# Column-tiled SSD reads and outputs placed in front of the adaLN units of a hybrid decoder layer

## The chip, the cores and the metric

The kernel runs on one core of one Trainium2 chip, as a single program. The metric is device time in microseconds, the median of the runs made. TensorE (PE in the profile, its weight loads PEld) multiplies, VectorE is DVE, ScalarE is ACT, GpSimd is POOL, and SyncE (SP) issues every transfer. Each engine works through its own queue in order.

## The reference, cut to what matters

One decoder layer is run for 256 prompt tokens and 8 sample sequences of 8 tokens (320 token columns in all). Each layer modulates its input by adaLN: six vectors come from `silu(c) @ w_ada`, with one row of `c` per sequence. The branch that the change touches is the Mamba-2 (SSD) branch:

```
per group g of 8 (8 heads of dim 64, state 128):
  x, B, C = silu(conv4(h @ w_in)) ; dt = softplus(...) ; cs = cumsum(dt * A)
  state read    y_t  = exp(cs_t) * (C_t . state)                      sample sequences: 8 stored states
  in the chunk  y_t += sum_s [ (C_t . B_s) * exp(cs_t - cs_s) * dt_s ] x_s
  state update  state = exp(cs_L) * state + sum_s dL_s x_s B_s^T
  y = (y + d_skip * x) * silu(z) ; rmsnorm per group ; times w_ssd_proj
```

Everything is float32. Large products are made as three single-pass products of a value split into a high and a low part (`fp32r`); small ones, the state reads, the outputs y and the adaLN units among them, are made in plain float32.

## The kernel before, in words

The large products run as a stream of weight halves. A half is a 128x1024 block of one weight array, loaded into a ring of four `raw` tiles (the adaLN weights use the same ring), split by ACT (`whi`, a cast) and DVE (`wlo`, a subtraction), in rings of three each. `quad_mm` takes two halves (a quad) and makes 48 products (`mm`): three matmuls for each of 4 column blocks `mb` and 4 rows `kk`. A stage of 16 quads is `project`, here over `w_sp` (for the first group over `w_gp`); a stage of 4 quads is one block of `w_in`. After each block `mb` of a half, eight times in a quad, `bg.tick()` advances a background generator by one step; a generator that yields n lets n ticks pass. Only TensorE's order is written by hand; the other engines' queues are ordered by a scheduler, and `now(x)` keeps an instruction behind the last TensorE instruction emitted before it.

Every second quad (`ada_every[0] = 2`) one adaLN unit is loaded at the start of the quad and multiplied at its end by `Ada.mm`: 4 matmuls of 128x512 in four column strips of 32 (`tile_position=(0, 32*j)`), after `flush` has transposed (`p`) the results of a finished row.

`ssd_work` is the generator of one group. It starts while the z columns of `w_in` are multiplied (4 quads) and goes on during the following `w_sp` stage of the group before. Its TensorE work stands between ticks: two state reads `inter` (4 strips of 32 each), eight updates `upd`, `cb` (C by B), the transposes `xT` and `bT`, the prompt state `fin` (two matmuls, with `bt`, copied by ACT, and `xL`, made by POOL), and four outputs `y`, one for each pair of heads, in two strips of 64. Before each y, ACT makes the weights of two heads in `weights(h)`: three Relu activations and one Exp, and POOL multiplies by `cb`. In the z stage ACT also evacuates the four products of z as `silu` (`evac_z`); the first products of the following stage need the same four PSUM buffers. Exp and silu stand in different ACT tables, and a change of table is an instruction (`ACT_TABLE_LOAD`).

In the line numbers of the profile: L115 is every matmul, L118 every transpose, L132 the cast `whi`, L106 every two-operand operation of DVE or POOL, L109 every activation, L167 a weight load.

Of the kernel before, what the change touches and what calls it, by code (L numbers as in the profile page):

```python
# [19 lines left out]
NT = 320  # L20
# [40 lines left out]
def hybrid_kernel(tc, ctx, a, o):  # L61
# [71 lines left out]
        return first, tt(eng, lo, src, hi.bitcast(F32), ALU.subtract)  # L133


    class Background:
        def __init__(self):
            self.queue = []
# [2 lines left out]
        def add(self, gen):  # L141
            self.queue.append(gen)

        def tick(self):
            if self.wait > 0:
                self.wait -= 1
                return
            if self.queue:
                try:
                    self.wait = next(self.queue[0]) or 0  # L150
                except StopIteration:
                    self.queue.pop(0)
# [95 lines left out]
    class Ada:  # L248
# [23 lines left out]
                self.loaded.append((c, b0, nb, q, raws))  # L272

        def mm(self):
            self.flush()
            if not self.loaded:
                return
            c, b0, nb, q, raws = self.loaded.pop(0)
            if q == 0:
                t = psum.tile([128, 512], F32, tag="ad", bufs=1, name="ad")  # L280
                self.ps = t
            w = 128 * nb
            m = 2048 // w
            n = m // len(raws)
            for j in range(m):
                T.matmul(self.ps[32 * (j % 4):32 * (j % 4) + 32, :w], c_s[:, m * q + j, :],
                         raws[j // n][:, (j % n) * w:(j % n) * w + w], start=q == 0 and j < 4,
                         stop=q == nb - 1 and j >= m - 4, tile_position=(0, 32 * (j % 4)))
            if q == nb - 1:
                part = stile([128, 512], name="adap")  # L290
                S.copy(part[:, :w], self.ps[:, :w])
                self.parts.append((c, b0, nb, part))
# [31 lines left out]
        T.matmul(ps, wh, xl, start=False, stop=False)  # L324
        T.matmul(ps, wl, xh, start=False, stop=stop)

    def quad_mm(pss, name, xq, first, last, evac, n_ada, apart, later):
        xh, xl = xq
        if n_ada:
            ada.load()  # L330
        for h in range(2):
            wh, wl = stream.take(name + (h,))
            for mb in range(4):
                for k2 in range(2):
                    kk = 2 * h + k2
                    c = k2 * 512 + mb * 128
                    block(pss[mb][:, :NT], wh[:, c:c + 128], wl[:, c:c + 128],
                          xh[:, kk], xl[:, kk], first and kk == 0, last and kk == 3)
                if mb == 0:
                    stream.ahead(1 if apart and last and h == 1 else S_AHEAD)  # L340
                if h == 0 and mb == 1 and later is not None:
                    later()
                if last and h == 1 and evac is not None:
                    evac(mb, pss)
                bg.tick()
        if n_ada:
            ada.mm()

# [3 lines left out]
    def gemm(names, quads, evac, apart=False):  # L352
        pss = [mm_ps() for _ in range(4)]
        n = len(names)
        for q in range(n):
            quad_no[0] += 1
            xq = quads(q) if callable(quads) else quads[q]
            quad_mm(pss, names[q], xq, q == 0, q == n - 1, evac,
                    1 if ada_every[0] and len(ada.units) > 4 and quad_no[0] % ada_every[0] == 0 else 0, apart,
                    (lambda: quads(q + 1)) if callable(quads) and q + 1 < n else None)  # L360


# [601 lines left out]
    def v8(x):  # L964
        return x.rearrange("p (h d) -> p h d", d=64)
# [4 lines left out]
    def ssd_work(W):  # L970
# [19 lines left out]
        xl = stile([64, 512], name="xl")  # L990
        tt(V, v8(xl), v8(ps[0:64]), bc8(dtL_tok[:, hsl]), ALU.mult)
        tt(V, v8(xs_tok[0:64]), v8(ps[0:64]), bc8(dt_tok[0:64, 2, hsl]), ALU.mult)
        yield 4

        psA = ax_ps("inter")
        for hf in range(2):
            mv = stack_v(xl, hf)
            states.read(psA, [cpad[:, 4 * hf + j] for j in range(4)], hf, hf == 0, hf == 1)
            for j in range(4):
                st = states.tiles[4 * hf + j]  # L1000
                tt(G, v8(st), v8(st), bc8(ecs_all[:, hsl, 4 * hf + j]), ALU.mult)
            if hf == 0:
                csb = []
                for i in range(2):
                    t = qtile(name="csb")
                    src = bass.AP(tensor=cs_d.tensor, offset=cs_d.offset + (8 * g + 4 * i) * NT,
                                  ap=[[0, 128], [NT, 4], [1, NT]])
                    now(nc.sync.dma_start(t, src))
                    csb.append(t)
            yield 1  # L1010
            for j in range(4):
                states.update(hf, j, hst[hf][:, j], mv, lambda st, ps: tt(V, st, st, ps, ALU.add))
                yield 1
        inter = stile([128, 512], name="inter")
        tt(V, v8(inter), v8(psA), bc8(ecs_r[:, hsl]), ALU.mult)
        yield 1
        states.store(8)

        ps = ax_ps("cb")
        T.matmul(ps[:, 0:256], Bc[:, 0:128], Cc[:, 0:256], start=True, stop=True)  # L1020
        T.matmul(ps[:, 256:384], Bc[:, 128:256], Cc[:, 128:256], start=True, stop=True)
        wide = W.bcm.rearrange("p a b -> p (a b)")[:, NT * 2 * (g % 2) + NP:NT * 2 * (g % 2) + NP + 128]
        T.matmul(ps[:, 384:448], wide, Cc[:, 256:320], start=True, stop=True)
        cb = stile([128, 448], name="cb")
        tt(V, cb[:, 0:384], ps[:, 0:384], mask[:, 0:384], ALU.mult)
        tt(V, cb[0:64, 384:448], ps[0:64, 384:448], mask[0:64, 384:448], ALU.mult)

        wt = ws[0:64]
        for i in range(2):
            now(tt(V, wt[:, 4 * i:4 * i + 4], csb[i][0:64, :, NP:],  # L1030
                   cs_tok[0:64, 2, 8 * g + 4 * i:8 * g + 4 * i + 4].unsqueeze(2).to_broadcast([64, 4, 64]),
                   ALU.subtract))
        V.tensor_scalar(out=wt, in0=wt, scalar1=0.0, scalar2=None, op0=ALU.min)
        act(wt, wt, AF.Exp)
        tt(V, wt, wt, cb[0:64, 384:448].unsqueeze(1).to_broadcast([64, 8, 64]), ALU.mult)
        yield

        xdt = []
        for tb in range(2):
            ps = ax_ps("xT")  # L1040
            for mb in range(4):
                T.transpose(ps[:, 128 * mb:128 * mb + 128], xs[:, mb, 128 * tb:128 * tb + 128], ident)
            xt = stile([128, 512], name="xdt")
            tt(V, v8(xt), v8(ps), bc8(dt_tok[:, tb, hsl]), ALU.mult)
            xdt.append(xt)
            yield

        ps = ax_ps("bT")
        for tb in range(2):
            T.transpose(ps[:, 128 * tb:128 * tb + 128], Bc[:, 128 * tb:128 * tb + 128], ident)  # L1050
        bt = stile([128, 2, 128], name="bt")
        S.copy(bt, ps[:, 0:256].rearrange("p (a b) -> p a b", a=2))
        xL = []
        for tb in range(2):
            xl = stile([128, 512], name="xL")
            tt(G, v8(xl), v8(xdt[tb]), bc8(dL_tok[:, tb, hsl]), ALU.mult)
            xL.append(xl)
        yield 3
        ps = ax_ps("fin")
        for tb in range(2):  # L1060
            T.matmul(ps, bt[:, tb], xL[tb], start=tb == 0, stop=tb == 1)
            yield
        fs = stile([128, 512], name="fs")
        S.copy(fs, ps)
        nc.sync.dma_start(o["ssm_p"][g], fs)


        def weights(h):
            cbr = csb[h // 4][:, h % 4]
# [6 lines left out]
            tt(G, w, w, cb[:, 0:384], ALU.mult)  # L1076
            return w

        ahead = [weights(0), weights(1)]
        yield 4  # L1080
        for j in range(4):
            if j < 3:
                ahead += [weights(2 * j + 2), weights(2 * j + 3)]

            ps = ax_ps("y")
            w = [ahead.pop(0), ahead.pop(0)]
            for cols, lhs, rhs, first in (
                    (slice(0, 256), xdt[0], lambda e: w[e][:, 0:256], True),
                    (slice(128, 256), xdt[1], lambda e: w[e][:, 256:384], False),
                    (slice(256, 320), xs_tok, lambda e: ws[:, 2 * j + e], True),  # L1090
                    (slice(256, 320), inter, lambda e: sel, False)):
                for e in range(2):
                    h = 2 * j + e
                    T.matmul(ps[64 * e:64 * e + 64, cols], lhs[:, 64 * h:64 * h + 64], rhs(e), start=first,
                             stop=not first, tile_position=(0, 64 * e))
            i = 4 * g + j
            V.scalar_tensor_tensor(out=xs[:, j], in0=xs[:, j], scalar=vec[:, V_DS + i:V_DS + i + 1],
                                   in1=ps[:, :NT], op0=ALU.mult, op1=ALU.add)
            yield 4

    def ssd_finish(W):
        g, xs = W.g, W.xs
# [332 lines left out]
```

## Time and profile before

| | |
|---|---|
| median of 3 runs | 2919.72 us (2915.18 to 2924.14) |
| the profiled execution, its own time | 2921.36 us |
| its span, first to last instruction | 2919.6 us |
| mean granted TensorE clock | 0.995 |
| PE busy | 2867.7 us (98%) |
| DVE, ACT, POOL busy | 1582.2 us (54%), 1237.1 us (42%), 377.5 us (13%) |

TensorE sets the time: whatever lengthens or shortens its queue by a microsecond, or lets it wait, shows in the total. The other engines have spare time on average, but their queues are in order, so that one late instruction holds back what stands behind it.

### The profile page before, as it was taken

What the parts mean: (1) busy time and instruction counts of PE and PEld (TensorE: products, weight loads), DVE (VectorE), ACT (ScalarE), POOL (GpSimd) and SP (SyncE); (2) the same over time, 40 slices, a digit from 0 to 9 for tenths busy, and PEclk for the clock granted to TensorE, in tenths of its full rate; (3) what the DMA queues carried; (4) which work ended last, traced back from release to release, by engine and by line L of the source; (5) the groups of instructions that cost most, each with busy time, mean ns of one, the idle gap of its engine ahead of it and who ended that gap; (6) DMA issues with size and microseconds to landing.
All of it is one profiled execution on the core that took longest, in us unless ns stands there. A gap on an engine that the chain in (4) does not pass through costs nothing.

```text
span 2919.6 us, 48446 instructions
## 1 busy us (share of the span) xinstructions
PE 2867.7 (98%) x19596; PEld 2685.1 (92%) x19596; DVE 1582.2 (54%) x2302; ACT 1237.1 (42%) x1954; POOL 377.5 (13%) x517
## 2 busy tenths in 40 slices
PE   7999999999999999999999999999999999999998
PEld 5899789998989989889888999999999999999998
DVE  4666555756646666666565554456434444444445
ACT  4344544344554554545454343335333333333333
POOL 0002121213322232323223000000000000000000
PEclk9999999999999999999999999999999999999999
DMA  9847636657676675776757554464444444444443
GB/s 381 324 146 240 200 127 219 225 173 271 223 242 236 217 260 192 255 242 201 255 197 251 195 170 159 165 212 145 152 149 148 151 152 149 148 151 151 149 149 116
DMA packets 181111, 575.54 MB, mean 197 GB/s; under 512 B 23252, under 2 KB 24600, under 8 KB 180888
## 3 DMA queue, kind: packets, MB, share of 16 engines
q1 hardware_dynamic: 180888, 572.45, 57.6%
q8 instruction: 154, 2.52, 0.3%
q14 instruction: 69, 0.57, 0.1%
HBM read 528.63 MB, written 43.74 MB: 196 GB/s over the span
## 4 chain that ended last, share of the span: by engine, by line
PE 52%; DVE 1%; issue 1%; DMA 0%; ACT 0%; POOL 0%; DVEq 0%; SPq 0%; ACTq 0%
PE mm L115 50%; PE ad L115 1%; DMA raw<-w_sp 0%; PE y L115 0%; DVE cacc L945 0%; DVE x L106 0%; PE sum L115 0%; DVE wlo L106 0%; PE fin L115 0%; PE upd L115 0%; PE inter L115 0%; DVE x L1183 0%; ACT whi L132 0%; PE xT L118 0%; DVE cacc L942 0%
## 5 line engine op out<-in xcount | busy, mean ns | idle before, releaser
L106 DVE TENSOR_TENSOR wlo<-raw,whi 128x1024 fp32r<-128x1024 f32 x712 | 879.9, 1238 | 931.2 <-ACT whi L132 920.4
L132 ACT CAST whi<-raw 128x1024 fp32r<-128x1024 f32 x712 | 745.9, 1048 | 1387.1 <-PE mm L115 1020.9
L115 PE MATMUL mm<-hh,whi 128*128 128x320 f32 x2560 | 813.2, 318 | 2.9 <-ACT hh L132 2.0
L115 PE MATMUL mm<-hh,wlo 128*128 128x320 f32 x2560 | 791.7, 309 | 1.7 <-DVE wlo L106 1.4
L115 PE MATMUL mm<-hl,whi 128*128 128x320 f32 x2560 | 790.8, 309 | 1.3 <-DVE hl L106 1.3
L115 PEld LDWEIGHTS mm<-hh,whi 128*128 128x128 f32 x2560 | 481.1, 188 | 82.1 <-issue 38.1
L115 PEld LDWEIGHTS mm<-hl,whi 128*128 128x128 f32 x2560 | 481.6, 188 | 10.2 <-issue 2.9
L115 PEld LDWEIGHTS mm<-hh,wlo 128*128 128x128 f32 x2560 | 481.3, 188 | 2.6 <-DVE wlo L106 2.5
L115 PE MATMUL mm<-gh,whi 128*128 128x320 f32 x1408 | 435.2, 309 | 0.8 <-ACT gh L1257 0.8
L115 PE MATMUL mm<-gl,whi 128*128 128x320 f32 x1408 | 435.4, 309 | 0.0
L115 PE MATMUL mm<-gh,wlo 128*128 128x320 f32 x1408 | 435.1, 309 | 0.0
L115 PEld LDWEIGHTS mm<-gh,whi 128*128 128x128 f32 x1408 | 264.4, 188 | 1.8 <-ACT gh L1257 1.8
L115 PEld LDWEIGHTS mm<-gl,whi 128*128 128x128 f32 x1408 | 264.4, 188 | 0.5 <-DVE gl L106 0.3
L115 PEld LDWEIGHTS mm<-gh,wlo 128*128 128x128 f32 x1408 | 264.4, 188 | 0.0
L115 PE MATMUL mm<-ahi,whi 128*128 128x320 f32 x704 | 217.5, 309 | 0.0
L115 PE MATMUL mm<-alo,whi 128*128 128x320 f32 x704 | 217.5, 309 | 0.0
L115 PE MATMUL mm<-ahi,wlo 128*128 128x320 f32 x704 | 217.5, 309 | 0.0
L106 POOL TENSOR_TENSOR ss<-ss,sq 128x320 f32<-128x320 f32 x14 | 12.7, 911 | 1392.9 <-ACT sq L109 1392.8
L115 PE MATMUL mm<-yhi,whi 128*128 128x320 f32 x512 | 170.2, 332 | 0.2
L115 PE MATMUL mm<-yhi,wlo 128*128 128x320 f32 x512 | 158.2, 309 | 0.0
L115 PE MATMUL mm<-ylo,whi 128*128 128x320 f32 x512 | 157.9, 308 | 0.0
L115 PEld LDWEIGHTS mm<-ahi,whi 128*128 128x128 f32 x704 | 132.2, 188 | 0.0
(281 smaller groups left out, 3623.2 us busy)
## 6 DMA issues: line engine op xcount, KB each, us to landing
raw<-w_in SPq DMA_DIRECT2D x320, 512.0 KB, 3.8
raw<-w_fi SPq DMA_DIRECT2D x176, 512.0 KB, 3.6
raw<-w_ada SPq DMA_DIRECT2D x120, 512.0 KB, 5.7
raw<-w_fo SPq DMA_DIRECT2D x88, 512.0 KB, 3.5
raw<-w_sp SPq DMA_DIRECT2D x64, 512.0 KB, 5.1
araw<-w_ada SPq DMA_DIRECT2D x52, 512.0 KB, 8.3
st<-S_gla SPq DMA_DIRECT2D x64, 256.0 KB, 5.4
gla_s<-st SPq DMA_DIRECT2D x64, 256.0 KB, 4.7
```

The costliest lines, as they stand in the source:

```text
L106: return eng.tensor_tensor(out=out, in0=in0, in1=in1, op=op)
L115: Tensor.last = nc.tensor.matmul(*args, **kw)
L132: first = S.copy(hi, src)
```

## The change

Three things are done. (1) A generator may yield `UNIT`: it is then resumed only at the tick at the end of every second quad, directly in front of the place of an adaLN unit. (2) `Ada.mm` issues its unit first and the transposes of an earlier row afterwards. (3) In `ssd_work` both state reads and the outputs wait for `UNIT`; the outputs are made in four strips of 32 columns and two pairs at a time, so that there are two such places in a group and not four. What stood between the reads and the outputs is placed anew: `cb`, the `xT` transposes and the weights of heads 0 and 1 come between the two reads, the weights of heads 2 and 3 behind the second read's updates and ahead of `bT` and `fin`, those of heads 4 to 7 between the two output places. `yield 3` between `bT` and `fin` is now `yield 1`.

```
-        def tick(self):
-            if self.wait > 0:
+        def tick(self, unit=False):
+            if self.wait == UNIT and not unit:
+                return
+            if self.wait != UNIT and self.wait > 0:
                 self.wait -= 1
                 return
...
         def mm(self):
+            old, self.parts = self.parts, []
+            self.unit()
+            new, self.parts = self.parts, old
             self.flush()
+            self.parts = new
...
-                bg.tick()
+                bg.tick(h == 1 and mb == 3 and slot)
...
+        yield UNIT
         psA = ax_ps("inter")
         for hf in range(2):
             mv = stack_v(xl, hf)
...
+            if hf == 0:
+                cb = products()
+                yield
+                for tb in range(2):
+                    token_major(tb)
+                    yield
+                ahead += [weights(h) for h in range(2)]
+                yield UNIT
         inter = stile([128, 512], name="inter")
         tt(V, v8(inter), v8(psA), bc8(ecs_r[:, hsl]), ALU.mult)
         yield 1
         states.store(8)
...
+        sample_weights()
+        ahead += [weights(h) for h in range(2, 4)]
         ps = ax_ps("bT")
...
-        yield 3
+        yield 1
         ps = ax_ps("fin")
...
+        for p in range(2):
+            yield UNIT
+            for j in (2 * p, 2 * p + 1):
+                ps = ax_ps("y")
...
+                    for e in range(2):
+                        for c in (0, 32):
+                            at = 64 * e + c
+                            T.matmul(ps[at:at + 32, cols], lhs[:, 128 * j + at:128 * j + at + 32], rhs(e),
+                                     start=first, stop=not first, tile_position=(0, at))
...
+            if p == 0:
+                ahead += [weights(h) for h in range(4, 8)]
+        yield 1
```

TensorE, the outputs of one group, before: two of the four places, with an adaLN unit between them. `mm` is a product of the stage, `y` an output, `ad` an adaLN unit.

```order
L115 MATMUL y<-w,xdt 64x256 x2
L115 MATMUL y<-w,xdt 64x128 x2
L115 MATMUL y<-ws,xs_tok 64x64 x2
L115 MATMUL y<-cst,inter 64x64 x2
...
L115 MATMUL ad<-raw,c_s 32x512 x4
```

The same place in the change:

```order
L115 MATMUL mm<-yhi,wlo 128x320
L115 MATMUL y<-w,xdt 32x256 x4
L115 MATMUL y<-w,xdt 32x128 x4
L115 MATMUL y<-ws,xs_tok 32x64 x4
L115 MATMUL y<-cst,inter 32x64 x4
...
L115 MATMUL ad<-raw,c_s 32x512 x4
L118 MATMUL p_15477<-erl,adap 128x128 x4
L115 MATMUL mm<-yhi,whi 128x320
```

All 32 outputs of the program stand so afterwards, two at a time, and all 16 state reads stand directly ahead of an `ad`. Before, every output stood alone between products; of the reads 8 stood alone, 4 directly ahead of an `ad` and 4 ahead of one with a transpose `p` between them.

ACT, group 5, around the start of the `w_sp` stage, before. `z` is the evacuation of the z products, the two `whi` are the first and the second half of `w_sp`, `w` are head weights.

```order
L109 ACTIVATE z_13158<-mm_13159 128x320
L109 ACTIVATE z_13158<-mm_13160 128x320
L132 CAST whi_13436<-raw_13434 128x1024
L109 ACTIVATE z_13158<-mm_13161 128x320
L109 ACTIVATE z_13158<-mm_13162 128x320
L132 CAST whi_13482<-raw_13480 128x1024
L291 COPY adap_13520<-ad_12949 128x512
```

The same stretch in the change:

```order
L109 ACT_TABLE_LOAD
L109 ACTIVATE w_13633<-w_13633 128x384
L132 CAST whi_13603<-raw_13601 128x1024
L109 ACTIVATE w_13639<-csb_13502,nd_tok_86 128x128
L109 ACTIVATE w_13639<-csb_13502,cs_tok_85 128x128
L132 CAST whi_13659<-raw_13657 128x1024
L109 ACTIVATE w_13639<-w_13639 128x384
L109 ACT_TABLE_LOAD
L109 ACTIVATE z_13318<-mm_13319 128x320
```

The four evacuations of z moved behind the casts of both halves, behind the Exp of head 1 and behind a table load.

ACT, group 5, from the fourth half of `w_sp` to `fin`, before; the fifth half is `whi_13640`.

```order
L132 CAST whi_13570<-raw_13568 128x1024
L109 ACT_TABLE_LOAD
L109 ACTIVATE ws_90<-ws_90 64x512
L1052 COPY bt_13647<-bT_13644 128x256
L132 CAST whi_13640<-raw_13638 128x1024
L132 CAST whi_13679<-raw_13677 128x1024
L1064 COPY fs_13701<-fin_13684 128x512
```

The same stretch in the change; the fifth half is `whi_13805`.

```order
L132 CAST whi_13805<-raw_13803 128x1024
L109 ACTIVATE w_13822<-csb_13502,cs_tok_85 128x128
L109 ACTIVATE w_13822<-csb_13502,nd_tok_86 128x128
L109 ACTIVATE w_13822<-csb_13502,cs_tok_85 128x128
L109 ACTIVATE w_13828<-csb_13502,cs_tok_85 128x128
L109 ACT_TABLE_LOAD
L109 ACTIVATE w_13822<-w_13822 128x384
L109 ACTIVATE ws_90<-ws_90 64x512
L109 ACTIVATE w_13828<-csb_13502,nd_tok_86 128x128
L109 ACTIVATE w_13828<-csb_13502,cs_tok_85 128x128
L1089 COPY bt_13837<-bT_13834 128x256
```

The copy `bt` stood ahead of the fifth cast and stands now behind it, behind the weights of heads 2 and 3 and a table load. POOL's queue at the same place, first before, then in the change:

```order
L106 TENSOR_TENSOR xL_13649<-xdt_13608,dL_tok_87 128x512
L106 TENSOR_TENSOR xL_13651<-xdt_13622,dL_tok_87 128x512
L106 TENSOR_TENSOR w_13704<-w_13704,cb_13588 128x384
```

```order
L106 TENSOR_TENSOR w_13822<-w_13822,cb_13588 128x384
L106 TENSOR_TENSOR xL_13839<-xdt_13612,dL_tok_87 128x512
L106 TENSOR_TENSOR xL_13841<-xdt_13625,dL_tok_87 128x512
L106 TENSOR_TENSOR w_13828<-w_13828,cb_13588 128x384
```

The weights of head 2 stand now ahead of both `xL`. In the change these pieces read alike in all eight groups (in the second one copies of `yb` stand between). On TensorE the first `fin` stood 78 products behind the start of the `w_sp` stage, with `cb`, the `xT` and `bT` transposes and one `upd` ahead of it; in the change it stands 72 products behind it, with four `upd` and `bT` ahead of it.

## Rows read from the trace of the kernel before

**Rows 1.** The page, part 1: busy time of each engine, share, instructions.
```profile
PE 2867.7 (98%) x19596; PEld 2685.1 (92%) x19596; DVE 1582.2 (54%) x2302; ACT 1237.1 (42%) x1954; POOL 377.5 (13%) x517
```

**Rows 2.** Timeline of PE, one output: start us, us, engine, line, operation, out<-in.
```profile
1328.93 0.31 PE L115 MATMUL mm<-yhi,wlo 128*128 128x320 f32 x1
1329.17 0.87 PE L115 MATMUL y<-w,xdt 128*64 128x256 f32 x8
1329.88 0.28 PE L115 MATMUL y<-ws,xs_tok 128*64 128x64 f32 x4
1329.99 0.29 PE L115 MATMUL y<-cst,inter 128*64 128x64 f32 x4
...
1330.46 0.31 PE L115 MATMUL mm<-ylo,whi 128*128 128x320 f32 x1
```

**Rows 3.** Timeline of PE, a state read that stands alone.
```profile
1297.41 0.31 PE L115 MATMUL mm<-hh,wlo 128*128 128x320 f32 x1
1297.65 1.06 PE L115 MATMUL inter<-st,cpad 128*32 128x512 f32 x8
...
1298.90 0.30 PE L115 MATMUL mm<-hl,whi 128*128 128x320 f32 x1
```

**Rows 4.** Timeline of PE, a state read directly ahead of an adaLN unit.
```profile
796.24 0.31 PE L115 MATMUL mm<-hh,wlo 128*128 128x320 f32 x1
796.48 1.07 PE L115 MATMUL inter<-st,cpad 128*32 128x512 f32 x8
797.36 1.04 PE L115 MATMUL ad<-raw,c_s 128*32 128x512 f32 x8
...
798.59 0.31 PE L115 MATMUL mm<-hl,whi 128*128 128x320 f32 x1
```

**Rows 5.** Timeline of PE, start of the w_sp stage in group 5.
```profile
1305.83 0.41 PE L115 MATMUL mm<-yhi,whi 128*128 128x320 f32 x1
1306.09 0.30 PE L115 MATMUL mm<-ylo,whi 128*128 128x320 f32 x1
...
1307.69 0.40 PE L115 MATMUL upd<-mv,hs 96*128 96x512 f32 x1
1307.94 0.31 PE L115 MATMUL mm<-yhi,whi 128*128 128x320 f32 x1
```

**Rows 6.** Timeline of ACT, group 5, first z and second half.
```profile
1301.83 0.44 ACT L109 ACTIVATE z<-mm 128x320 f32<-128x320 f32 x1 [3.23 <-PE mm L115]
...
1305.29 1.05 ACT L132 CAST whi<-raw 128x1024 fp32r<-128x1024 f32 x1
```

**Rows 7.** Timeline of ACT, group 5, table load, fifth half, weights of heads.
```profile
1312.60 1.28 ACT L109 ACT_TABLE_LOAD   x1
...
1318.04 1.05 ACT L132 CAST whi<-raw 128x1024 fp32r<-128x1024 f32 x1 [0.66 <-DMA raw<-w_sp]
...
1322.86 0.40 ACT L109 ACTIVATE w<-csb,cs_tok 128x128 f32<-128x128 f32 x1
...
1324.04 0.52 ACT L109 ACTIVATE w<-w 128x384 f32<-128x384 f32 x1
```

**Rows 8.** Groups of POOL by form: count, busy us, mean ns, idle before.
```profile
L106 POOL TENSOR_TENSOR w<-w,cb 128x384 f32<-128x384 f32 x64 | 69.2, 1085 | 92.6 <-issue 46.4 <-ACT w L109 44.6 <-DMA raw<-w_ada 1.5
...
L106 POOL TENSOR_TENSOR xL<-xdt,dL_tok 128x512 f32<-128x512 f32 x16 | 23.4, 1475 | 110.2 <-DVE xdt L106 110.1
```

**Rows 9.** Timeline of POOL, group 5.
```profile
1317.20 2.49 POOL L106 TENSOR_TENSOR xL<-xdt,dL_tok 128x512 f32<-128x512 f32 x2 [13.37 <-DVE xdt L106]
```

**Rows 10.** Stretches: length, busy of PE, PEld, DVE, ACT, POOL, clock, DMA, GB/s.
```profile
293.00:305.50 12.50, 6.92 (x25) 3.81 (x25) 7.97 (x9) 6.61 (x12) 6.80 (x7) 1.00 0.11 43
305.50:308.90 3.40, 3.40 (x15) 3.40 (x14) 0.27 (x1) 0.00 (x0) 0.00 (x0) 0.50 0.00 0
...
1414.00:1418.00 4.00, 2.60 (x18) 2.33 (x17) 4.00 (x7) 1.68 (x7) 0.00 (x0) 1.00 0.97 290
```

**Rows 11.** Timeline of PE, waits and then products at the lower clock.
```profile
301.96 0.42 PE L115 MATMUL mm<-ohi,whi 128*128 128x320 f32 x1 [1.63 <-ACT ohi L132]
303.95 0.42 PE L115 MATMUL mm<-olo,whi 128*128 128x320 f32 x1 [1.57 <-DVE olo L106]
...
305.85 0.47 PE L115 MATMUL mm<-ohi,wlo 128*128 128x320 f32 x1
306.11 0.47 PE L115 MATMUL mm<-ohi,whi 128*128 128x320 f32 x1
```

More of the change, by code (lines that the diff above doesn't have):

```diff
@@ L133, in split @@
         return first, tt(eng, lo, src, hi.bitcast(F32), ALU.subtract)
+    UNIT = "unit"
     class Background:
@@ L274, in mm, with unit @@
         def mm(self):
+            old, self.parts = self.parts, []
+            self.unit()
+            new, self.parts = self.parts, old
             self.flush()
+            self.parts = new
+        def unit(self):
             if not self.loaded:
@@ L325, in block, with quad_mm @@
         T.matmul(ps, wl, xh, start=False, stop=stop)
-    def quad_mm(pss, name, xq, first, last, evac, n_ada, apart, later):
+    def quad_mm(pss, name, xq, first, last, evac, slot, apart, later):
+        n_ada = slot and len(ada.units) > 4
         xh, xl = xq
@@ L358, in gemm @@
             quad_mm(pss, names[q], xq, q == 0, q == n - 1, evac,
-                    1 if ada_every[0] and len(ada.units) > 4 and quad_no[0] % ada_every[0] == 0 else 0, apart,
+                    ada_every[0] > 0 and quad_no[0] % ada_every[0] == 0, apart,
                     (lambda: quads(q + 1)) if callable(quads) and q + 1 < n else None)
@@ L992, in ssd_work, with products, sample_weights, token_major @@
         tt(V, v8(xs_tok[0:64]), v8(ps[0:64]), bc8(dt_tok[0:64, 2, hsl]), ALU.mult)
-        yield 4
+        csb, xdt, ahead = [], [], []
+        def products():
+            ps = ax_ps("cb")
+            T.matmul(ps[:, 0:256], Bc[:, 0:128], Cc[:, 0:256], start=True, stop=True)
+            T.matmul(ps[:, 256:384], Bc[:, 128:256], Cc[:, 128:256], start=True, stop=True)
+            wide = W.bcm.rearrange("p a b -> p (a b)")[:, NT * 2 * (g % 2) + NP:NT * 2 * (g % 2) + NP + 128]
+            T.matmul(ps[:, 384:448], wide, Cc[:, 256:320], start=True, stop=True)
+            cb = stile([128, 448], name="cb")
+            tt(V, cb[:, 0:384], ps[:, 0:384], mask[:, 0:384], ALU.mult)
+            tt(V, cb[0:64, 384:448], ps[0:64, 384:448], mask[0:64, 384:448], ALU.mult)
+            return cb
+        def sample_weights():
+            wt = ws[0:64]
+            for i in range(2):
+                now(tt(V, wt[:, 4 * i:4 * i + 4], csb[i][0:64, :, NP:],
+                       cs_tok[0:64, 2, 8 * g + 4 * i:8 * g + 4 * i + 4].unsqueeze(2).to_broadcast([64, 4, 64]),
+                       ALU.subtract))
+            V.tensor_scalar(out=wt, in0=wt, scalar1=0.0, scalar2=None, op0=ALU.min)
+            act(wt, wt, AF.Exp)
+            tt(V, wt, wt, cb[0:64, 384:448].unsqueeze(1).to_broadcast([64, 8, 64]), ALU.mult)
+        def token_major(tb):
+            ps = ax_ps("xT")
+            for mb in range(4):
+                T.transpose(ps[:, 128 * mb:128 * mb + 128], xs[:, mb, 128 * tb:128 * tb + 128], ident)
+            xt = stile([128, 512], name="xdt")
+            tt(V, v8(xt), v8(ps), bc8(dt_tok[:, tb, hsl]), ALU.mult)
+            xdt.append(xt)
+        def weights(h):
+            cbr = csb[h // 4][:, h % 4]
+            hh = 8 * g + h
+            w = pool.tile([128, 384], F32, tag="w", bufs=4, name="w")
+            now(act(w[:, 0:128], cbr[:, 0:128], AF.Relu, scale=-1.0, bias=cs_tok[:, 0, hh:hh + 1]))
+            now(act(w[:, 128:256], cbr[:, 128:256], AF.Relu, scale=-1.0, bias=nd_tok[:, hh:hh + 1]))
+            now(act(w[:, 256:384], cbr[:, 128:256], AF.Relu, scale=-1.0, bias=cs_tok[:, 1, hh:hh + 1]))
+            act(w, w, AF.Exp, scale=-1.0)
+            tt(G, w, w, cb[:, 0:384], ALU.mult)
+            return w
+        yield UNIT
         psA = ax_ps("inter")
@@ L1002, in ssd_work @@
             if hf == 0:
-                csb = []
                 for i in range(2):
@@ L1012, in ssd_work @@
                 states.update(hf, j, hst[hf][:, j], mv, lambda st, ps: tt(V, st, st, ps, ALU.add))
-                yield 1
+                if j < 3:
+                    yield 1
[7 more added lines that the diff above has]
+                yield UNIT
         inter = stile([128, 512], name="inter")
@@ L1017, in ssd_work @@
         states.store(8)
[L1019 to L1046, printed above, removed]
+        sample_weights()
+        ahead += [weights(h) for h in range(2, 4)]
         ps = ax_ps("bT")
@@ L1065, in ssd_work @@
         nc.sync.dma_start(o["ssm_p"][g], fs)
-        def weights(h):
-            cbr = csb[h // 4][:, h % 4]
-            hh = 8 * g + h
-            w = pool.tile([128, 384], F32, tag="w", bufs=4, name="w")
-            now(act(w[:, 0:128], cbr[:, 0:128], AF.Relu, scale=-1.0, bias=cs_tok[:, 0, hh:hh + 1]))
-            now(act(w[:, 128:256], cbr[:, 128:256], AF.Relu, scale=-1.0, bias=nd_tok[:, hh:hh + 1]))
-            now(act(w[:, 256:384], cbr[:, 128:256], AF.Relu, scale=-1.0, bias=cs_tok[:, 1, hh:hh + 1]))
-            act(w, w, AF.Exp, scale=-1.0)
-            tt(G, w, w, cb[:, 0:384], ALU.mult)
-            return w
@@ L1079, in ssd_work @@
[L1079 to L1099, printed above, removed]
+        for p in range(2):
+            yield UNIT
+            for j in (2 * p, 2 * p + 1):
+                ps = ax_ps("y")
+                w = [ahead.pop(0), ahead.pop(0)]
+                for cols, lhs, rhs, first in (
+                        (slice(0, 256), xdt[0], lambda e: w[e][:, 0:256], True),
+                        (slice(128, 256), xdt[1], lambda e: w[e][:, 256:384], False),
+                        (slice(256, 320), xs_tok, lambda e: ws[:, 2 * j + e], True),
+                        (slice(256, 320), inter, lambda e: sel, False)):
+                    for e in range(2):
[3 more added lines that the diff above has]
+                                     start=first, stop=not first, tile_position=(0, at))
+                i = 4 * g + j
+                V.scalar_tensor_tensor(out=xs[:, j], in0=xs[:, j], scalar=vec[:, V_DS + i:V_DS + i + 1],
+                                       in1=ps[:, :NT], op0=ALU.mult, op1=ALU.add)
+            if p == 0:
+                ahead += [weights(h) for h in range(4, 8)]
@@ L1101, in ssd_finish @@
+        yield 1
     def ssd_finish(W):
```

## The prediction

> **What bounds the kernel now.** I read the page's busy shares first. TensorE is busy 98% of the span [rows 1], so the sum is made on its queue. Next I read its timeline around the blocks that the change touches. A product of the stage follows the one before after 0.1455 us (eleven steps from 1306.09 to 1307.69 in [rows 5]). What a block costs is then the time from the last product ahead of it to the second product behind it, less two steps (0.29). By that an output costs 1330.46 - 1328.93 - 0.29 = 1.24 us [rows 2], a state read that stands alone 1298.90 - 1297.41 - 0.29 = 1.20 us [rows 3], and a read with an adaLN unit directly behind it 798.59 - 796.24 - 0.29 = 2.06 us [rows 4]. So the second block of the same mode adds 0.86 us, and 1.20 - 0.86 = 0.34 us of a block alone is getting into the mode and out of it. Last I read the timelines of ACT and POOL, since the new order moves ACT's and POOL's instructions more than TensorE's.
>
> **What the change gives: 15.0 us.** By the order on TensorE, 32 outputs that stood alone now adjoin an adaLN unit. So do the 8 reads that stood alone, and the 4 reads that had a transpose between. That is 44 times 0.34 us = 15.0 us. The outputs keep 1.24 - 0.34 = 0.90 us each in this sum. No row shows an output in four strips. From below it takes the 0.86 us of a read, which streams 512 columns a strip as an output does (256 + 128 + 64 + 64): the gain would be 16.3. From above it takes the fastest pace of records shown, 4 in 0.11 us (1329.88 to 1329.99, [rows 2]). An output has now eight records of each of four kinds, which at that pace take 0.22 us at least; the widest kind, 256 columns, takes 0.43, half of the 0.86 of 512. That makes 0.43 + 3 x 0.22 = 1.09 us, and a gain of 15.0 - 32 x 0.19 = 8.9 us. I stay at 0.90, near the read, because eight records in four strips are what [rows 4] show at full stream.
>
> The Trainium skill, page "TensorE: Matmul & The Clock Gate", section "Wait — 56ns, not 53.3ns?", speaks against the narrow strips: from one matmul's start to the next it finds never less than about 25 ns, however few columns. By that the two kinds of 64 columns would take 0.20 us each, an output an estimated 1.04 us and the gain an estimated 10.5 us; the 27 ns of the row is the nearest that this trace has.
>
> Moving `p` behind its unit costs nothing by itself: the same transposes stand on TensorE. The wait for `UNIT` delays work inside a group, but the group's ticks end before the next group needs its result, and the order shows the generators finished in the same stages; the cover is the w_sp stage of 768 products, and if a group were drained at its end, the blocks would merely stand alone again.
>
> **What it costs: two waits in each group, together 6.8 us.** Both come from what stands ahead in an in-order queue. I count from the start of the w_sp stage (1305.83, [rows 5]), where TensorE would be without any wait.
>
> When `fin` is due. Ahead of it stand 72 products (10.5 us), four updates of 0.25 us (1307.69 to 1307.94), a first step that is 0.11 longer (0.26, [rows 5]) and two short transposes, for which I add 0.2: 11.8 us after the stage's start.
>
> When `fin` can start. It needs `xL`, which now stands on POOL behind the weights of head 2, which wait for ACT's Exp of head 2. On ACT this Exp stands behind the cast of the fifth half, four Relus and a table load. That cast starts at 1318.04, which is 12.2 us after the stage's start, and the row says what it waited for: the load of that half [rows 7]. The ring of raw tiles is not changed, so I leave it there. From then on: cast 1.05; four Relus 1.18 (1322.86 to 1324.04); table load 1.28; Exp 0.52 [rows 7]; POOL's product with `cb` 1.09 [rows 8]; the first `xL` 1.25, half of the two [rows 9]. Sum 12.2 + 6.4 = 18.6 us. So TensorE is 18.6 - 11.8 = 6.8 us late when `fin` has started. Behind it on TensorE stand the whole stream's products, and nothing else can run there.
>
> Part of the 6.8 us is paid earlier. The first product of the stage needs z's first PSUM buffer. Its evacuation ran at 1301.83, 4.0 us ahead of the stage's start; now it stands on ACT behind the cast of the second half. That cast started at 1305.29, 0.54 us ahead of the stage. From there 1.05 for the cast, 0.52 for the Exp of head 1, 1.28 for the table load back to silu and 0.44 for z [rows 6, 7] end 2.75 us after the stage was due to start. The rest, 4.05 us, is the wait at `fin`. A shorter first wait makes the second longer by as much, as long as the fifth half's load sets the second.
>
> The bounds. The fifth cast takes the buffer of the second half, which TensorE gives back after 48 products and three updates, 7.9 us after the start. If the load were not late, `fin` could start at 7.9 + 6.4 = 14.3, and 2.5 us would be lost in a group. With POOL at the slower mean of `xL` (1.48, [rows 8]) it is 7.0 us. Over eight groups: 20 to 56 us, taken 54.4.
>
> **The clock.** After waits of 1.6 us twice within 4 us [rows 11] the granted clock stood at 0.50 (1.2 GHz) for 3.4 us, where TensorE had been busy 6.9 of 12.5 us; one stretch with 1.4 us of idle time in 4 did not lower it [rows 10]. At the lower level a product follows after 0.26 us (305.85 to 306.11), so such a time costs 3.4 x (1 - 0.1455/0.26) = 1.5 us. A wait of 4 us is longer than those. I take one such time in each group: 12.0 us; the bounds are none and two in each group, 0 and 24 us.
>
> **The sum.** 2921.4 - 15.0 + 54.4 + 12.0 = 2972.8 us against the profiled execution. That one stood 1.6 us above the median, so the median would be 2971 us.
>
> **The rivals.**
> - The mode is shared and the waits are hidden: faster. For it: ACT is busy 42% and POOL 13% [rows 1], and every instruction that was added has room on average. The mechanism decides at one point: `xL` must be ready 11.8 us after the stage's start, so the fifth cast must start at 11.8 - 6.4 = 5.4 us. Against it: the buffer comes free only at 7.9, and in the profile the load comes at 12.2. It would give 2921.4 - 15.0 = 2906.4, as a median 2905 us.
> - Both waits come, but the clock holds: 2960.8, as a median 2959 us. For it: the stretch around 1414 in [rows 10].
> - The load is early and only the short wait remains: 2921.4 - 15.0 + 20 = 2926 us without the clock, up to 2938 with it.
> - The narrow strips run at the pace of the records: 6 us more than each of these cases.
> - That the change doesn't bring blocks together is out: the order shows each of the 32 outputs and 16 reads beside a unit.
>
> **How the numbers follow.** Both waits with a lower clock in most groups 0.52, with the clock held 0.23, short waits 0.13 (0.06 of it within 0.3%, the rest slower), the slow strips on top of the long waits with two falls of the clock 0.04, hidden waits 0.08. A change of 0.3% (8.8 us) is about what three runs that spread by 9 us can tell from none. So: faster 0.08, same 0.06, slower 0.86. The likeliest case gives 2971. The range leaves out the hidden waits below and the sum of all upper ends above: from 2930, inside the short waits (2926 to 2938), to 2994, the long waits (56 us) with outputs at 1.09 and two falls of the clock in most groups.
>
> **What would show it.** In the profile of the changed kernel an output pair beside its unit should add about 1.8 us (two of 0.90). The read beside a unit should stay at 2.06. In every group TensorE should idle ahead of the first product of the w_sp stage for about 2.7 us, with ACT's z as releaser, and ahead of the first `fin` for about 4 us, with POOL's `xL`; the clock should show 0.5 behind some of these. I am wrong if `fin` starts without a wait: then either the fifth half lands much earlier than before, or ACT works in another order than the program's. I am wrong in size if the fifth cast starts later or earlier than 12 us after the stage's due start, since every microsecond there is 8 us in the total, or if the low clock covers more than 3.4 us of work at a time.

## The result and the profile after

The changed kernel takes 2968.76 us (median of 4 runs, 2963.76 to 2972.05) against 2918.12 us for the kernel before, run beside it (4 runs, 2915.18 to 2924.14): a ratio of 1.017, 95% interval 1.0158 to 1.0181. It is 50.6 us slower; the forecast was 2971. The profiled execution has a span of 2969.6 us, 50.0 more than before, and a mean granted clock of 0.987.

Part 1 of the page answers to [rows 1].

```profile
PE 2867.9 (97%) x20108; PEld 2690.0 (91%) x20108; DVE 1587.0 (53%) x2302; ACT 1260.6 (42%) x1970; POOL 368.3 (12%) x517
```

TensorE has the same busy time as before in a span that is 50 us longer, so the added time is idle time. That the busy time is the same is two things offsetting each other: in the version with the operands made early, below, which has the same matmuls and no low clock among the groups, it is 2851.6 us, 16 less, and the matmuls that the changed kernel makes at the low clock take about as much longer. The list of TensorE's waits says for what it stood idle (us in total, times, longest).

```profile
PE fin L115 <- POOL xL L106: 42.3, 8, 5.8
...
PE xT L118 <- DVE cb L106: 6.6, 4, 2.4
PE mm L115 <- ACT z L109: 3.6, 5, 1.0
```

In the list of before none of the three stands. The timeline of TensorE in group 5, from the second read over the start of the `w_sp` stage to the first two outputs, answers to [rows 2, 4, 5].

```profile
1336.59 0.31 PE L115 MATMUL mm<-hh,wlo 128*128 128x320 f32 x1
1336.83 1.06 PE L115 MATMUL inter<-st,cpad 128*32 128x512 f32 x8
1337.71 1.04 PE L115 MATMUL ad<-raw,c_s 128*32 128x512 f32 x8
1339.23 0.41 PE L115 MATMUL mm<-yhi,whi 128*128 128x320 f32 x1 [0.47 <-ACT z L109]
1339.48 0.31 PE L115 MATMUL mm<-ylo,whi 128*128 128x320 f32 x1
...
1348.13 0.38 PE L115 MATMUL mm<-yhi,whi 128*128 128x320 f32 x1 [0.65 <-DVE yb L106]
...
1351.80 0.31 PE L115 MATMUL mm<-yhi,wlo 128*128 128x320 f32 x1
1357.15 2.08 PE L115 MATMUL fin<-xL,bt 128*128 128x512 f32 x2 [5.05 <-POOL xL L106]
...
1359.56 0.47 PE L115 MATMUL mm<-yhi,wlo 128*128 128x320 f32 x1
1359.83 0.47 PE L115 MATMUL mm<-yhi,whi 128*128 128x320 f32 x1
...
1362.03 0.31 PE L115 MATMUL mm<-ylo,whi 128*128 128x320 f32 x1
1362.18 0.31 PE L115 MATMUL mm<-yhi,wlo 128*128 128x320 f32 x1
...
1365.30 0.29 PE L115 MATMUL y<-ws,xs_tok 128*32 128x64 f32 x8
1365.41 0.29 PE L115 MATMUL y<-cst,inter 128*32 128x64 f32 x8
1365.52 0.83 PE L115 MATMUL y<-w,xdt 128*32 128x256 f32 x16
```

ACT and POOL in the same stretch answer to [rows 6, 7, 9].

```profile
1335.97 1.03 ACT L132 CAST whi<-raw 128x1024 fp32r<-128x1024 f32 x1
1336.91 0.52 ACT L109 ACTIVATE w<-w 128x384 f32<-128x384 f32 x1
1337.44 1.28 ACT L109 ACT_TABLE_LOAD   x1
1338.74 1.42 ACT L109 ACTIVATE z<-mm 128x320 f32<-128x320 f32 x4
...
1350.52 1.05 ACT L132 CAST whi<-raw 128x1024 fp32r<-128x1024 f32 x1 [4.19 <-DMA raw<-w_sp]
...
1352.76 1.28 ACT L109 ACT_TABLE_LOAD   x1
1354.06 0.52 ACT L109 ACTIVATE w<-w 128x384 f32<-128x384 f32 x1
```

```profile
1354.66 0.99 POOL L106 TENSOR_TENSOR w<-w,cb 128x384 f32<-128x384 f32 x1 [11.44 <-ACT w L109]
1355.61 2.49 POOL L106 TENSOR_TENSOR xL<-xdt,dL_tok 128x512 f32<-128x512 f32 x2
```

The chain reads downwards: the fifth half's cast waits for its load and starts at 1350.52; Relus, table load, Exp; POOL's product with `cb`; the first `xL`, half of 2.49 us; `fin` at 1357.15. Meanwhile TensorE had stood since 1351.95. The stretches of 3.4 us around that wait (columns as in [rows 10]) show what follows.

```profile
1351.20:1354.60 3.40, 0.91 (x7) 0.64 (x5) 1.55 (x2) 3.37 (x8) 0.00 (x0) 1.00 0.73 253
1354.60:1358.00 3.40, 0.85 (x1) 0.50 (x2) 1.73 (x2) 2.70 (x6) 3.34 (x3) 0.50 0.30 99
1358.00:1361.40 3.40, 3.40 (x9) 2.27 (x8) 1.67 (x2) 0.00 (x0) 2.04 (x2) 0.50 0.31 99
1361.40:1364.80 3.40, 3.40 (x24) 2.89 (x26) 1.05 (x3) 0.80 (x2) 0.00 (x0) 1.00 0.37 134
```

The clock falls to 1.2 GHz while TensorE waits and stays there for 3.4 us in which it is busy throughout, with 9 matmuls where the next 3.4 us hold 24.

**The account.** Measured as in the prediction (last product ahead of a block to the second one behind it, less two steps) and summed over the program: the blocks `fin` cost 71.0 us in place of 13.7. Of these 57.3 us the listed waits are 42.3, and the remaining 15.0 are put down to the low clock. The `xT` transposes cost 17.9 in place of 10.6, so 7.3 more. The reads ahead of a unit hold 4.0 us of waiting for z beyond their bare 2.05. The outputs fell from 39.4 us to 28.0, the reads by 8 x 0.34 + 4 x 0.33 = 4.0. That makes 57.3 + 7.3 + 4.0 - 15.4 = 53.2 us. The spans differ by 50.0, so this is 3 us too much. Some 2 of them are waits of before that are smaller or gone (`upd` for DVE's `st` 0.9 us in place of 2.9, `bT` for `cb` 1.0, a product for `wlo` 1.4), less 2.5 us of new waits for `yb`; the rest is open.

### The profile page after: what moved, and what is told of

Same layout as the page of the kernel before. It is cut to its first block, busy times and chain, and to the rows that moved or that the text cites. A ratio compares the mean times of both kernels' runs of the same rounds, so it can differ in the third digit from the quotient of the medians.

```text
span 2969.6 us, 49526 instructions
## 1 busy us (share of the span) xinstructions
PE 2867.9 (97%) x20108; PEld 2690.0 (91%) x20108; DVE 1587.0 (53%) x2302; ACT 1260.6 (42%) x1970; POOL 368.3 (12%) x517
## 4 chain that ended last, share of the span: by engine, by line
PE 84%; issue 5%; DMA 4%; DVE 3%; POOL 2%; ACT 1%; SPq 0%; DVEq 0%; ACTq 0%; POOLq 0%
PE mm L115 75%; DMA raw<-w_in 3%; PE ad L115 2%; PE fin L115 1%; POOL st L106 1%; PE y L115 1%; DVE wlo L106 1%; PE inter L115 1%; PE upd L115 1%; ACT whi L132 1%; PE o L115 1%; POOL w L106 1%; DVE cacc L956 0%; PE att L115 0%; PE sum L115 0%
## 5 line engine op out<-in xcount | busy, mean ns | idle before, releaser
L106 DVE TENSOR_TENSOR wlo<-raw,whi 128x1024 fp32r<-128x1024 f32 x712 | 889.5, 1251 | 986.4 <-ACT whi L132 978.8
L115 PEld LDWEIGHTS mm<-ahi,wlo 128*128 128x128 f32 x704 | 132.1, 188 | 0.0
```

The costliest lines, as they stand in the source:

```text
L106: return eng.tensor_tensor(out=out, in0=in0, in1=in1, op=op)
L115: Tensor.last = nc.tensor.matmul(*args, **kw)
```

## Experiments

All times are medians; a ratio is that to runs of the kernel before on the same chip, with its 95% interval. The first four kernels start from the changed kernel and change one place of the source each; the order of the other engines' queues can follow.

**The weights of heads 2 and 3 behind `xL`.**

```
-        ahead += [weights(h) for h in range(2, 4)]
...
             xL.append(xl)
+        ahead += [weights(h) for h in range(2, 4)]
         yield 1
```

> The weights of heads 2 and 3 are issued behind bT, bt and both xL; nothing else is changed, so POOL makes xL without waiting for an Exp. Theory (fin is late because of what stands ahead of xL on ACT and POOL): in group 5 of the changed kernel fin was due 12.9 us after the first product of the w_sp stage and the fifth cast began 11.3 us after it; fin now needs only cast 1.05, one Relu 0.40 and bt 0.35 behind that, 13.1 us, so the wait falls from 5.3 us (mean of eight) to below 1 us and ACT's bt becomes its releaser. The total falls by 8 x 5 = 40 us and by what the low clock behind the wait costs, which I estimate at 17 us (6.8 us at 0.50, of which some 2 lie in the wait itself, 4.8 x (1 - 0.1455/0.26) = 2.1 us in each group): 2968.8 - 57 = 2912 us. Rival 1 (the low clock comes from the waits for z and xT too, and stays): 2929 us. Rival 2 (POOL is late for another reason than the Exp, such as xdt): no change, 2969 us.

Measured: 2924.15 us (10 runs), ratio 1.0012 (0.9998 to 1.0026). TensorE's waits:

```profile
PE xT L118 <- DVE cb L106: 5.0, 3, 2.0
PE mm L115 <- ACT z L109: 4.2, 5, 1.4
PE fin L115 <- ACT bt L1088: 3.7, 5, 0.9
```

POOL is gone as a releaser of `fin`, ACT's `bt` behind the fifth cast has taken its place as foreseen, and the clock stands low only once among the groups, for 3.4 us. Moving one line returns 44.6 of the 50.6 us: the queue ahead of `xL` was the cause. The missing 12 us to the 2912 of the theory are mostly waits that it did not count. The outputs with their units cost 52.8 us in place of 48.6, since they now wait for POOL's `w` (their weight loads, 3.2 us in 8 places), and `fin` still costs 6 us more than bare.

**`fin` 30 products later.** `yield 1` ahead of `fin` becomes `yield 6`.

> yield 6 in place of yield 1 between bT and fin: fin stands 30 products further back on TensorE, 30 x 0.1455 = 4.4 us; ACT and POOL keep their order up to xL. Theory (xL is ready at a time of its own, and TensorE only comes too early): the wait at fin falls from 5.3 to 0.9 us, the clock stays at full speed behind it, and the total is 2968.8 - 8 x 4.4 - 17 = 2917 us. Rival (what xL waits for moves back with TensorE, since its buffers come free by TensorE's work): the wait stays near 5 us and the total near 2969 us.

Measured: 2951.72 us, ratio 1.0117 (1.0101 to 1.0133); neither number. The blocks `fin` cost 15.4 us, so that the theory's first half holds: `xL` is ready at a time of its own. But the longest entry in the list of waits is now another:

```profile
PE mm L115 <- DVE wlo L106: 27.9, 7, 5.3
```

In group 4 the outputs stand at 1258.3 and 1275.4, 32.9 and 50.0 us behind the start of the `w_sp` stage (1225.4), where the changed kernel has 25.2 and 42.3. `fin` had slipped past the first unit's place, and each pair went one place further. This corrects the prediction's cover: a stage over `w_sp` has 4 quads, 192 products or 28 us, and two places; the "16 quads" and "768 products" in the texts ahead were wrong, and I had read them from no row. The second pair then falls into the next `w_in` block, and the end of the group meets the next group's convolution on DVE:

```profile
1292.16 2.15 DVE L380 RECIPROCAL rstd<-rstd 128x320 f32<-128x320 f32 x1 [0.62 <-ACT rstd L109]
...
1302.49 2.04 DVE L956 SCALAR_TENSOR_TENSOR cacc<-u,vec,cacc 128x344 f32<-128x344 f32 x4
1304.44 1.22 DVE L106 TENSOR_TENSOR wlo<-raw,whi 128x1024 fp32r<-128x1024 f32 x1
```

DVE works from 1292.16 to the `wlo` without a pause (rows left out), and TensorE waits 3.7 us for that `wlo`, 4 us on average in seven groups. The clock stood at 1.2 GHz at each of these seven waits, for 3.4 or 6.8 us. Waits and low clock together make the products cost 42 us more than in the changed kernel, against 55.7 that `fin` gives back; that about makes the 13.2 us between the spans of the two profiled executions.

**The weights of heads 0 and 1 behind `xL`**, those of heads 2 and 3 still ahead of it: the line `ahead += [weights(h) for h in range(2)]` is taken from between the reads and put behind `xL`.

> The weights of heads 0 and 1 move from between the two reads to behind xL; those of heads 2 and 3 stay ahead of xL. z is then evacuated without an Exp and its tables ahead of it, and the wait of 1.0 to 1.6 us at the start of the w_sp stage should vanish. The step of the prediction under test (a shorter first wait makes the second longer by as much, since the load of the fifth half sets the second): fin waits some 6.5 us in place of 5.3 and the total stays within 4 us of 2969. Rival (the fifth half follows what TensorE gives back, so all of it comes earlier): fin's wait stays at 5.3 and the total falls by 8 x 1.3 = 10 us to 2958.

Measured: 2968.62 us, ratio 1.0173 (1.0158 to 1.0188). The median is that of the changed kernel to 0.1 us, as the prediction's step says, though the wait for z is gone from the list. But `fin` did not wait longer for it (39.0 us in 8 places, against 42.3), and the profiled execution is 4.9 us shorter (2964.7). The exchange between the two waits is not shown, and the trace says why the run can't show it: the edit changed ACT's queue as well. Four Relus of the next weights now stand ahead of the fifth cast and not behind it, so that `fin` starts 5.6 us behind that cast in all eight groups, where the changed kernel has 6.6. The cast itself started 12.2 us behind the due start of the stage on average, against 11.6, so the load did not come sooner, as the rival wanted, and its 10 us did not come either.

**The wait filled with useless work.**

```
         ps = ax_ps("fin")
+        for _ in range(10):
+            T.matmul(ps[:, 0:256], Bc[:, 0:128], Cc[:, 0:256], start=True, stop=True)
```

> Ten products of B and C (128x256, plain float32) are put directly ahead of fin, into the PSUM tile that fin overwrites; they need nothing new. A 128x512 of this type took 0.59 us (fin at full clock, mean), so ten take about 10 x 0.59 / 2 = 3 to 4.5 us, less than the wait of 5.3. Added work inside a wait costs nothing by itself. Theory (the clock falls because TensorE idles there, and that costs time): the granted clock stays at 1.00 in most groups and the total falls by the price of the low clock, estimated at 17 us, to 2952. Rival 1 (the low clock costs next to nothing, since it lies over the wait): 2969 us. Rival 2 (the clock falls in any case): 0.50 stays for 6.8 us in each group, 2969 us or a little above.

Measured: 2950.24 us, ratio 1.011 (1.0095 to 1.0125): 18.5 us less than the changed kernel, for 80 matmuls more. Timeline and stretches of group 5:

```profile
1342.22 4.48 PE L115 MATMUL fin<-bcm 128*128 128x256 f32 x20
1347.87 1.12 PE L115 MATMUL fin<-xL,bt 128*128 128x512 f32 x2 [1.18 <-POOL xL L106]
```

```profile
1342.20:1347.80 5.60, 4.50 (x22) 3.62 (x20) 2.62 (x3) 5.57 (x13) 2.43 (x3) 1.00 0.47 172
1347.80:1354.60 6.80, 6.73 (x68) 5.28 (x72) 4.06 (x6) 2.13 (x5) 2.96 (x3) 1.00 0.37 118
```

The time until `fin` is nearly as long as before (5.2 us on average from the last product, against 5.6), but the clock stays at 2.4 GHz behind every `fin`, and the 6.8 us hold 68 matmuls. By blocks, `fin` and its filling cost 55.3 us where `fin` alone had cost 71.0. Of these 15.7 us some 3 are the earlier `fin` (8 x 0.35), so that the low clock cost the changed kernel about 13 us; the rest of the 18.5 is smaller waits that fell otherwise (`xT` 13.2 in place of 17.9, the reads with their units 33.1 in place of 28.6). The clock is still low twice elsewhere, for 3.4 us each, behind waits of 1.4 and 0.9 us close together and behind one of 1.8 us.

**The operands made early.** The outputs and reads keep their places; what they and `fin` need is made elsewhere: `bT`, `bt` and both `xL` between the reads, the weights of heads 0 to 3 behind the first two updates of the second read.

```
                 cb = products()
-                yield
-                for tb in range(2):
-                    token_major(tb)
-                    yield
-                ahead += [weights(h) for h in range(2)]
+                yield 2
+                token_major(0)
+                yield 1
+                token_major(1)
+                yield
+                ps = ax_ps("bT")
...
+                bt = stile([128, 2, 128], name="bt")
...
+                    t = stile([128, 512], name="xL")
...
                 yield UNIT
...
+                if hf == 1 and j < 2:
+                    ahead += [weights(2 * j + i) for i in range(2)]
...
-        yield 1
+        yield 2
         ps = ax_ps("fin")
```

> The places of the reads and the outputs stay as in the change. bT, bt and both xL are made between the two reads, behind the xT transposes; the weights of heads 0 to 3 follow behind the first two updates of the second read (behind z, ahead of the fifth cast); cb and xT stand 12 and 6 products further apart, so that DVE has time for cb. Theory (all that the change lost are waits made by what stands ahead of xL, z and xT; the shared mode's gain is there all the time): no wait at fin, none for z, none at xT, the clock stays; then the total is that of before less the gain, 2919.5 - 15 = 2904 us. Rival 1 (the outputs' places press the rest of the group: the wait turns up elsewhere, as wlo in the run with fin later): 2915 to 2930 us. Rival 2 (the gain was not there): 2919 us.

Measured: 2904.52 us (5 runs), ratio 0.9949 (0.9937 to 0.9961). All 16 `fin` blocks cost 0.86 us, all `xT` 0.44, no output waits, and between 600 and 1700 us the clock never falls. Part 1 of the page, and the outputs beside a unit:

```profile
PE 2851.6 (98%) x20108; PEld 2681.9 (92%) x20108; DVE 1592.7 (55%) x2302; ACT 1238.2 (43%) x1954; POOL 369.2 (13%) x517
```

```profile
1332.08 0.31 PE L115 MATMUL mm<-yhi,wlo 128*128 128x320 f32 x1
1332.32 0.86 PE L115 MATMUL y<-w,xdt 128*32 128x256 f32 x16
...
1333.97 0.29 PE L115 MATMUL y<-cst,inter 128*32 128x64 f32 x8
1334.09 1.04 PE L115 MATMUL ad<-raw,c_s 128*32 128x512 f32 x8
...
1335.31 0.30 PE L115 MATMUL mm<-hl,whi 128*128 128x320 f32 x1
```

Two outputs and a unit cost 1335.31 - 1332.08 - 0.29 = 2.94 us; 1.19 of it is the unit, 1.75 the pair. So the gain was there all the time, and this version is faster than both kernels (13.6 us, 0.5%, less than the kernel before).

**Two strips instead of four**, and **pairs apart from the unit**, both on that version. Their edits: the output's loop of before (two matmuls of 64 columns for each operand); and `yield 3` behind the outputs' `yield UNIT`. The 25 ns in the first text are those of the Trainium skill's page that the prediction weighs.

> As the run with the operands made early, but each output in two strips of 64 columns, as before the change; they still stand two at a time directly ahead of an adaLN unit in four strips. Theory (what costs 0.34 us is any change of tiling mode): each of the 16 pairs pays for a second change, 16 x 0.34 = 5.4 us more than that run, 2910 us if that has 2904. Rival (only a change from and to the full array costs, two strips and four live together): the same time as that run. Second rival (narrow matmuls have a floor, four strips of 32 cost more than two of 64): less than that run, by 32 x (1.04 - 0.90) = 4.5 us if the floor were the page's 25 ns.

> As the run with the operands made early, but each pair of outputs (four strips, two pairs at a time) follows the unit's place by 24 products instead of standing directly ahead of the unit. Theory (the neighbour of the same mode saves 0.34 us): 16 x 0.34 = 5.4 us more than that run, 2910 us if that has 2904; the pair alone costs 1.75 + 0.34 = 2.09 us. Rival (the saving comes from two outputs standing together and from four strips, the unit beside them gives nothing): the same time as that run, and a pair costs 1.75 us.

Measured: two strips 2911.38 us, ratio 0.9975 (0.9965 to 0.9985); apart 2912.74 us, 0.9979 (0.9969 to 0.9988). The pair in two strips:

```profile
1338.32 0.31 PE L115 MATMUL mm<-yhi,wlo 128*128 128x320 f32 x1
1338.56 0.87 PE L115 MATMUL y<-w,xdt 128*64 128x256 f32 x8
...
1340.26 0.29 PE L115 MATMUL y<-cst,inter 128*64 128x64 f32 x4
1340.48 1.06 PE L115 MATMUL ad<-raw,c_s 128*32 128x512 f32 x8
...
1341.72 0.30 PE L115 MATMUL mm<-hl,whi 128*128 128x320 f32 x1
```

The pair apart:

```profile
1326.93 0.31 PE L115 MATMUL mm<-yhi,wlo 128*128 128x320 f32 x1
1327.17 0.86 PE L115 MATMUL y<-w,xdt 128*32 128x256 f32 x16
...
1329.31 0.31 PE L115 MATMUL mm<-ylo,whi 128*128 128x320 f32 x1
```

Apart, a pair costs 2.08 us and not 1.75 (theory: 2.09): the neighbour saves 0.33 us, 16 x 0.33 = 5.3 of the 8.2 us between the two versions. Some 3 us more are waits in and behind one adaLN unit at 933 us (0.5 us for a load of `w_ada`, 1.5 for `whi`, 0.8 for `wlo`); what made them is open. In two strips, pair and unit cost 3.11 us, 0.17 more than in four. My expectation of 0.34 counted a whole way in and out; there is only one change more (64 to 32). Nor is all of the 0.17 that change: the two outputs themselves run 1340.26 - 1338.56 = 1.70 us to their last operand, with four strips 1333.97 - 1332.32 = 1.65, so that about 0.12 is left for it. The pairs make 16 x 0.17 = 2.7 us of the 6.9; most of the rest is waits of the updates for `mv` (5.2 us in 5 places), which I had not foreseen and whose cause is open. The Trainium skill, page "TensorEngine Tiling (Array Packing)", section "Tiling Modes", says that a change of mode drains the engine; the 0.12 us, found between two tiled modes too, agree with it.

**`cb` and `xT` close together again**, on the version with the operands early: 6 products between them, all other queues in the same order.

> As the run with the operands made early, but cb and the two xT follow each other by 6 products, as in the change (there 18 and 12); bT stays where it was, and ACT, POOL and DVE keep their order. Theory (the second xT finds no free PSUM tile, since the read's sum holds one of three and DVE has not yet read cb): the wait at xT returns, in the change 6.6 us in four places (7.3 us over the bare transposes in all), and the total is 2904.5 + 7 = 2911 us. Rival (the wait at xT only takes time that would be lost behind it): 2904.5 us.

Measured: 2908.28 us, ratio 0.9965 (0.9954 to 0.9977). The wait for `cb` came back in one place only (1.8 us), the `xT` blocks cost 12.9 in place of 10.6 us, and the intervals of the two versions overlap. It is inconclusive as to the total. The queue behind the wait shows in DVE's rows of the changed kernel. In the four groups in which `xT` waits, DVE takes a `wlo` between its two reads of `cb` and stands idle there until ACT's cast for it is done, 0.7 to 2.6 us; in the four others both reads come ahead of the `wlo`. In group 4 the second read is at 1218.67 and `xT` at 1219.03:

```profile
1217.53 1.23 DVE L106 TENSOR_TENSOR wlo<-raw,whi 128x1024 fp32r<-128x1024 f32 x1 [2.58 <-ACT whi L132]
```

Here DVE's order was the same in four groups, but the cast was late in only one of them (2.0 us idle), and that is the one place in which the wait came back. So the distance to `cb` alone does not make the wait.

## Why the prediction was right

**The gain of 15.0 us** came out at 11.4 + 4.0 = 15.4. Its parts held: 0.34 us for each way in and out, an output of 0.875 us (taken 0.90), a read of 0.86. The slow-strips bound did not come: eight matmul records of 64 columns take 0.11 us (1365.30 to 1365.41), so the kinds run at full stream. The rule of about 25 ns from start to start in "TensorE: Matmul & The Clock Gate" (the Trainium skill, section "Wait — 56ns, not 53.3ns?") would make 0.20; over four strips this trace contradicts it, with 14 ns on average. Each strip has two of the eight, 55 ns apiece, so that within one strip nothing here speaks against it. That the gain comes from the shared mode is shown by the pair apart and the pair in two strips.

**The loss of 6.8 us in a group.** In group 5 the stage was due at 1338.68 (1336.59 + 0.29 + 2.05, less the 0.25 of the first step). The fifth cast started 11.8 us after that (forecast 12.2), `fin` 18.5 (forecast 18.6), and without the two waits ahead of it TensorE would have been there at 11.9 (forecast 11.8). So 6.6 us were lost, and the cause is shown by the weights moved behind `xL` and by the early operands. In the eight groups `fin` started 17.3 to 19.5 us behind the due start, 18.25 on average: the fifth cast started at 11.6 on average (forecast 12.2), and from it to `fin` it was 6.63 us in every group (forecast 6.4).

**Its split was wrong.** The wait for z was to be 2.75 us and was 0.55 in group 5, 4.0 in all and not 22; the wait at `fin` was 42.3 us and not 32.4. The failed step is "That cast started at 1305.29, 0.54 us ahead of the stage". In [rows 6] that cast has no idle time ahead of it: it started there because z's evacuations stood ahead of it on ACT, and not because its data came then. With z moved behind it, it ran at 1335.97, 2.7 us ahead of the due start. The sum suffered little, since it hangs on the start of `fin` alone, and there the cast's 0.6 us and the queue's 0.25 offset each other in part. "A shorter first wait makes the second longer by as much" did not show either: in the three groups without a wait for z the fifth cast started 10.7 to 11.2 us behind the due start and `fin` waited 4.8 to 5.8 us, in the five others 10.8 to 12.9 and 4.7 to 5.8. The load of the fifth half is the releaser of its cast in all eight groups; what sets its time is open.

**The clock, 12.0 us,** was the right mechanism with too short a fall: 6.8 us in seven groups and 3.4 in one, where 3.4 was taken. In group 5 it began at 1354.60, so that 2.5 of the 6.8 us lie over the wait itself and cost nothing. The blocks give 15.0 us and the filled wait about 13, between the bounds 0 and 24.

**Not foreseen:** the wait of `xT` for `cb`, 7.3 us, since `cb` and both `xT` now stand between the two reads, while the read's sum `inter` holds one of the three PSUM tiles. The second `xT` so waits for the tile of `cb`, until DVE has read it, and in four groups DVE reads it late, behind a `wlo` (rows above). That the forecast came out 2 us from the measured 2969 is in part luck, because errors offset each other: z was 18.0 us too high, and `fin` 9.9, the clock 1 to 3 and `xT` 7.3 too low.

**The rivals.** Hidden waits is the early-operands version: its 2904.5 us against the forecast 2905 shows that the rest of the sum was right, and that only the place of the operands decided. The held clock is the filled wait: 2950.2, where 2959 was written. The early load did not come: it needed a fifth cast 7.9 us behind the due start, and the cast started at 10.7 to 12.9.

## What to carry to other kernels

Before a block is moved to a better place, write down for each of its operands the queue that it now stands in and the last thing ahead of it with a real wait; here one line, that of the weights of heads 2 and 3, cost 44.6 us, three times what the shared mode gives. An instruction whose row shows no idle time ahead of it started when its engine came to it, so its start may not be carried over to another order. A wait of about 5 us on TensorE cost here more than its length, as the clock was low behind it; where it could not be removed, spare matmuls in it paid (18.5 us).

## What the runs showed of the hardware

- Going from the full array into strips and back costs TensorE 0.33 to 0.34 us; a neighbour in the same strips saves it. A change between strips of 64 and of 32 costs about 0.12 us.
- At each of the eight waits of 4.7 to 5.8 us the clock fell to 1.2 GHz while TensorE still waited and stood there for 6.8 us (once 3.4); with useless matmuls in it (group 5: 4.5 of 5.6 us) it stayed at 2.4.
- In four strips, matmul records of 64 columns start 14 ns apart on average (8 in 0.11 us, two in each strip).
